# Four more pairs of tiles as seven products, parked attention outputs, and rooms of two lengths, in a one-layer decoder step

## The chip, the cores and the metric

The kernel runs on one core of a Trainium2 chip. The metric is the device time of one execution in microseconds: 1503.17 us, the median of 3 runs (1502.42 to 1503.85).

The engines are named as the profile names them: PE multiplies matrices into accumulators, PEld loads its weights, DVE is VectorE, ACT is ScalarE, POOL is GpSimd, and SP issues nearly all DMAs, in the order of the program.

## The reference

One layer for 528 prompt positions (16 meta tokens ahead of 512 tokens) and for 32 new tokens of eight running sequences: a half-step SwiGLU FFN, a mixer of gated linear attention and stick-breaking attention side by side, and a second half-step FFN, with RMS norms around each. Cut to what the change touches:

```python
h = x + 0.5 * rms_norm(swiglu(rms_norm(x, ffn1_pre_g), ffn1_w_gate, ffn1_w_up, ffn1_w_down), ffn1_post_g)
u = rms_norm(h, mix_pre_g)
q_a, k_a, v_a, gk_low, r_a, q_b, k_b, v_b, gate_a, gate_b = jnp.split(u @ w_in, offs, axis=-1)
o_a, s_new = gla_branch(q_a, k_a, v_a, g, s0, lead)
o_a = rms_norm(o_a, gla_norm_g).reshape(B, L, V_GLA) * jax.nn.silu(r_a)
o_b = sb_attend(q_b, keys, vals, sb_bias, q_off).reshape(B, L, SB_W)
m = jax.nn.sigmoid(gate_a) * (o_a @ w_o_gla) + jax.nn.sigmoid(gate_b) * (o_b @ w_o_sb)
h = h + rms_norm(m @ w_out, mix_post_g)
y = h + 0.5 * rms_norm(swiglu(rms_norm(h, ffn2_pre_g), ffn2_w_gate, ffn2_w_up, ffn2_w_down), ffn2_post_g)
```

The model width is 1024 and the FFN width 2816 (22 chunks of 128). Everything is float32.

## The kernel before

**Numbers.** Activations stand feature by token: tiles of 128 features by the tokens, in two halves of columns (280 + 280 in FFN1, 280 + 264 in the mixer as ordinary tiles, 272 + 272 in seven products). Each float32 operand is split into a high and a low part (`hi` on ACT, L661; `lo` = operand − `hi` on DVE, through the helper `tt` at L153), and each product is three matmuls: hi·hi, hi·lo, lo·hi.

**An ordinary tile** (`tile_steps`, L675 ff.) takes 128 output features of a weight matrix of 1024 rows: 8 steps, one for each chunk of 128 rows, of 6 matmuls (3 for each half of the columns). The FFN down tiles go by `k_steps` (L695 to L698) over 22 chunks in the three stretches `CUTS`, either with both halves of the columns or with one; a step of one half is 3 matmuls.

**Seven products** (`seven_steps`, L998; for the FFNs, L1188 and L1248) takes two tiles at once. The two tiles, the two halves of the 1024 rows and the two halves of the columns are a product of 2 by 2 blocks, done as seven block products and additions, with four accumulators: 14 steps of 6 matmuls. It needs sums of weight blocks (`weight_sums`, four sums of 512 columns on DVE), `hi` and `lo` of four quarter sets of weights (`parts_of`, `parted_lo`), sums of the activations (`usum`, in the mixer read back from `sums_dram` by `sums_back` and split by `sums_hi` and `sums_lo`), and additions that put the results together (`made`, `add`). `weights_at` puts the weight sums 10 to 8 steps ahead of a pair, and the quarters from 6 steps ahead to 6 steps into it. `gate_pair` does so for the gates `a` and `b`.

**The order is written by steps.** A matmul generator yields after each step, `step()` runs then, and whatever was put down by `later(d, f)` or `when(n, f)` for this step is issued behind it. So the lists of numbers (`F0`, `F1`, `SUMS_BACK`, `EARLY`, the pieces of `Weights`) set which instruction stands where on each engine.

**Weights** come by `st.fetch` (DMA on SP, L186; quarters for pairs, L621), asked up to `AHEAD` instructions before they are used, in the order of the list `st.todo`. `fetch_early` (L634) loads a piece of `w_in` ahead of the list, `h_again` (L1294) reads the residual back for the end of FFN1.

**The stages.** FFN1's gates and ups; FFN1 down by `order1`: tiles 0 and 1, the pair 2/3 ("S2"), then tiles 4 to 7 for the first half of the columns and 7 to 4 for the second; during the second the norms of the first half run (`g1.pieces`, delays `F0`), and after it those of the second half (`F1`). Their last part are the rank products `ranks` (L1667). Then nine stretches of 24 steps, in which attention pairs 0 to 7 and the four heads of the linear attention are worked off; in the ninth the gate tiles r0 to r2. The normed outputs of the linear attention (`oa`, eight tiles) stay in SBUF until the r tile with their number multiplies them by silu(r). Then the mixer by the list `MIXER`, whose steps are counted from its start: tiles r3 to r7, the products o0 to o7 (`out_a`, w_o_gla), gates a0 and a1 as ordinary tiles (`gate_a`), and the other a and b gates in pairs between the products p0 to p7. Between them stand the running sequences' attention over the cached pages: `Weights(0)` and `Weights(1)` make the attention weights of a half of the heads (a scan on DVE, L2174 ff., turned by PE, copied by DVE at L2199 and L2200), `sample_new` (L2229) uses them with the new values at step 9, and `sample_values` with the pages. Last come w_out and FFN2.

**Rooms.** `Arena` hands out stretches of SBUF. It has 25 chunks of 6 units of the same kind, and prefers the room that was given back longest ago by the count of gives. Pages of the cache come from a list of their own (`ring`).

## Time and profile before

| | |
|---|---|
| median of 3 runs | 1503.17 us |
| the profiled execution | 1503.28 us |
| its span | 1501.6 us, granted clock 0.999 |
| PE busy | 1492.8 us, 11941 instructions |
| DVE busy | 1090.2 us, 1940 instructions |
| ACT busy | 772.7 us, 1422 instructions |
| POOL busy | 73.4 us, 146 instructions |
| HBM read, written | 155.72 MB, 22.74 MB |

A time in a view is counted from the start of the span. A row of a timeline has start, length, engine, line, operation, output and input, and in brackets how long the engine stood idle before it and what ended that. A busy interval of PE covers the pipelined matmul (0.28 us and more), and neighbours overlap: the pitch from start to start is what one costs. A row of windows has for each engine busy time and the count of instructions, then the granted clock, the share of the DMA engines and GB/s.

### The profile page before, as it was taken

Reading aid. Unit: us, or ns where it says so; the run is one execution under the profiler, and the core shown is the slowest. Engines: PE = TensorE matmul, PEld = TensorE weight load, DVE = VectorE, ACT = ScalarE, POOL = GpSimd, SP = SyncE. Lnnn points to the kernel's source line nnn. Section 1 sums busy time; section 2 is a strip of 40 time slices with the busy share of each in tenths; the row PEclk is TensorE's granted clock in tenths of the full one; section 3 lists DMA queues with packets and bytes.
Section 4 is the critical chain, followed back from the end, with each engine's and each line's share of the span. In section 5 each row is a group of like instructions: output and inputs, shape, how many; then the busy total and the mean of one; then the engine's idle time right before and its main releaser. Section 6 shows DMA issues by size and latency. Waiting matters only on the chain.

```text
span 1501.6 us, 29825 instructions
## 1 busy us (share of the span) xinstructions
PE 1492.8 (99%) x11941; PEld 1442.1 (96%) x11941; DVE 1090.2 (73%) x1940; ACT 772.7 (51%) x1422; POOL 73.4 (5%) x146
## 2 busy tenths in 40 slices
PE   9999999999999999999999999999999999999998
PEld 8999999999999889999898999999999999999998
DVE  5888888853787866877776534977567898888544
ACT  6455454533655556556555443634564555455334
POOL 2000000000000011112111000000000000000000
PEclk9999999999999999999999999999999999999999
DMA  8133333337565474343555668335531333333253
GB/s 251 51 91 100 99 99 98 86 91 209 148 161 144 126 113 85 91 109 91 130 103 141 192 193 192 100 99 145 156 108 67 94 104 99 99 99 91 86 167 99
DMA packets 280525, 180.40 MB, mean 120 GB/s; under 512 B 10140, under 2 KB 260706, under 8 KB 280386
## 3 DMA queue, kind: packets, MB, share of 16 engines
q1 hardware_dynamic: 280082, 178.42, 44.0%
q8 instruction: 94, 1.54, 0.4%
q14 instruction: 45, 0.37, 0.1%
q0 software_dynamic: 288, 0.07, 0.0%
q10 hardware_dynamic: 16, 0.00, 0.0%
HBM read 155.72 MB, written 22.74 MB: 119 GB/s over the span
## 4 chain that ended last, share of the span: by engine, by line
PE 94%; DVE 3%; ACT 1%; DMA 1%; issue 0%; DVEq 0%; ACTq 0%; SPq 0%
PE acc L682 8%; PE acc L1248 8%; PE acc L1249 8%; PE acc L685 8%; PE acc L683 8%; PE acc L1250 8%; PE acc L695 7%; PE acc L698 7%; PE acc L696 7%; DVE room L153 2%; PE acc L1028 1%; PE acc L1029 1%; PE acc L1191 1%; PE acc L1030 1%; PE acc L1188 1%; PE acc L1189 1%
## 5 line engine op out<-in xcount | busy, mean ns | idle before, releaser
L153 DVE TENSOR_TENSOR lo<-raw,hi 128x1024 fp32r<-128x1024 f32 (+1 forms) x213 | 254.9, 1198 | 126.7 <-ACT hi L661 102.8
L153 DVE TENSOR_TENSOR room<-room,room 128x544 f32<-128x544 f32 (+17 forms) x413 | 259.1, 650 | 81.7 <-ACT room L761 14.0
L682 PE MATMUL acc<-room,hi 128*128 128x280 f32 (+1 forms) x928 | 271.7, 310 | 0.2 <-DVE room L156 0.2
L1248 PE MATMUL acc<-room,hi 128*128 128x280 f32 (+1 forms) x896 | 259.7, 290 | 0.0
L1249 PE MATMUL acc<-room,hi 128*128 128x280 f32 (+1 forms) x896 | 259.5, 290 | 0.0
L1250 PE MATMUL acc<-room,lo 128*128 128x280 f32 (+1 forms) x896 | 259.2, 289 | 0.0
L683 PE MATMUL acc<-room,hi 128*128 128x280 f32 (+1 forms) x928 | 250.8, 289 | 0.0
L685 PE MATMUL acc<-room,lo 128*128 128x280 f32 (+1 forms) x928 | 193.0, 289 | 0.0
L682 PEld LDWEIGHTS acc<-room,hi 128*128 128x128 f32 x928 | 174.7, 188 | 13.0 <-issue 11.0
L683 PEld LDWEIGHTS acc<-room,hi 128*128 128x128 f32 x928 | 175.2, 189 | 2.8 <-issue 1.9
L1250 PEld LDWEIGHTS acc<-room,lo 128*128 128x128 f32 x896 | 168.7, 188 | 0.0
L1249 PEld LDWEIGHTS acc<-room,hi 128*128 128x128 f32 x896 | 168.6, 188 | 0.0
L1248 PEld LDWEIGHTS acc<-room,hi 128*128 128x128 f32 x896 | 168.5, 188 | 0.0
L959 ACT CAST hi<-raw 128x1024 fp32r<-128x1024 f32 x92 | 96.4, 1052 | 133.6 <-PE acc L1249 49.2
L661 ACT CAST hi<-raw 128x1024 fp32r<-128x1024 f32 (+1 forms) x121 | 122.6, 1014 | 70.9 <-DMA raw<-in_ffn_w_down_dram 20.8
L685 PEld LDWEIGHTS acc<-room,lo 128*128 128x128 f32 x928 | 145.2, 189 | 0.0
L695 PE MATMUL acc<-room,hi 128*128 128x280 f32 (+2 forms) x498 | 142.9, 294 | 0.4 <-ACT hi L661 0.4
L696 PE MATMUL acc<-room,hi 128*128 128x280 f32 (+2 forms) x498 | 140.9, 290 | 0.0
L698 PE MATMUL acc<-room,lo 128*128 128x280 f32 (+2 forms) x498 | 127.8, 291 | 0.7 <-DVE lo L153 0.7
L959 ACT CAST hi<-room 128x1024 fp32r<-128x1024 f32 x84 | 70.2, 836 | 81.1 <-PE acc L1249 60.5
L695 PE MATMUL acc<-room,room 128*128 128x280 f32 (+3 forms) x366 | 107.8, 295 | 0.0
L153 DVE TENSOR_TENSOR lo<-room,hi 128x1024 fp32r<-128x1024 f32 x84 | 80.2, 955 | 36.8 <-ACT hi L959 36.6
(400 smaller groups left out, 3222.4 us busy)
## 6 DMA issues: line engine op xcount, KB each, us to landing
raw<-in_w_in_dram SPq DMA_DIRECT2D x49, 512.0 KB, 7.1
raw<-in_ffn_w_down_dram SPq DMA_DIRECT2D x40, 448.0 KB, 4.0
raw<-in_ffn_w_gate_dram SPq DMA_DIRECT2D x64, 256.0 KB, 3.2
raw<-in_ffn_w_up_dram SPq DMA_DIRECT2D x64, 256.0 KB, 3.2
out_dram<-room SPq DMA_DIRECT2D x36, 256.0 KB, 4.8
room<-in_cache_k_dram SPq DMA_DIRECT2D x32, 256.0 KB, 3.8
room<-in_cache_v_dram SPq DMA_DIRECT2D x32, 256.0 KB, 4.7
raw<-in_ffn_w_down_dram SPq DMA_DIRECT2D x14, 512.0 KB, 4.2
```

The lines of the kernel that those rows point to most:

```text
L153: (eng or V).tensor_tensor(out=out, in0=a, in1=b, op=op)
L661: S.copy(h_, src)
L682: T.matmul(acc[h][:, : wid[h]], hi[k], a[h][0], start=(k == 0), stop=False)
L683: T.matmul(acc[h][:, : wid[h]], hi[k], a[h][1], start=False, stop=False)
L685: T.matmul(acc[h][:, : wid[h]], lo[k], a[h][0], start=False, stop=(k == KD - 1))
L695: T.matmul(acc[h][:nw, : wid[h]], wh, a[h][0], start=(k == 0), stop=False)
L696: T.matmul(acc[h][:nw, : wid[h]], wh, a[h][1], start=False, stop=False)
L698: T.matmul(acc[h][:nw, : wid[h]], wl, a[h][0], start=False, stop=(k == kt - 1))
L959: S.copy(hi[:, :kt], src)
L1248: T.matmul(x[:, :QW], hi, act[k][0], start=(first and k == 0), stop=False, skip_group_check=True)
L1249: T.matmul(x[:, :QW], hi, act[k][1], start=False, stop=False, skip_group_check=True)
L1250: T.matmul(x[:, :QW], lo, act[k][0], start=False, stop=(k == 3), skip_group_check=True)
```

## The change

It does the following; how the order moves is shown at three places below.

- **Four more pairs as seven products.** In FFN1 down, tiles 4 and 5 ("S4" in `order1`), right behind the pair 2/3; of its 22 chunks, eight go as seven products, the others as before. In the mixer, r3/4 and r5/6 (the new `r_pair`) and the gates a0/1 (`gate_pair`; `gate_a` is gone).
- **The mixer's order.** `MIXER` now begins 24 steps earlier in its own count, with r0, r1, r2 in the last of the nine stretches; then r7, the two r pairs, o0 to o3, a0/1, o4, o5, a2/3, o6, o7, and the rest. The first product o0 reads its eight inputs in the order 0, 1, 2, 7, 3, 4, 6, 5.
- **The sums of the activations** (`sums_back`) are read back and split during attention pairs 5 to 8 instead of at steps 80 to 104 of the mixer. The first half of the full tiles of u is given back in parts when r3/4 begins.
- **Parking.** Each head of the linear attention stores its two outputs in `oa_dram` and gives their rooms back; r0, r1, r2 and r7 load theirs when they begin, an r pair 6 steps after it begins (`oa_back`).
- **FFN1 down's end.** Only tiles 6 and 7 are left as single ones. `F0` and `LATE` have other delays, the early piece of `w_in` goes from tile 4 to tile 7, and `h_again` starts 14 steps after pair 4/5 (pieces of another size) instead of 2 steps after pair 2/3.
- **Weights(0)** has its scans two steps and its turning and copies three steps later. The 16 small copies of `sample_out` go from DVE to ACT. The loads of `ob` and of pages have fixed steps.
- **Rooms.** 20 chunks of 6 units and the rest of 2; a room freed 14 steps ago or more is preferred; pages use the same rooms.

In the programs, PE has 48 matmuls less (11398 to 11350). DVE has 37 two-operand instructions more and the 16 copies less, SP 18 DMAs more (575).

PE, at step 8 of the mixer. In both programs the rows of `ps` are `sample_new(0)`, ahead of it are the last of the tile before and one step of the next. Before:

```order
L685 MATMUL acc_9609<-room_20_279,lo_9400 128x280
L685 MATMUL acc_9610<-room_20_279,lo_9400 128x264
L682 MATMUL acc_9716<-room_15_160,hi_9533 128x280
L683 MATMUL acc_9716<-room_15_160,hi_9533 128x280
L682 MATMUL acc_9717<-room_15_160,hi_9533 128x264
L683 MATMUL acc_9717<-room_15_160,hi_9533 128x264
L685 MATMUL acc_9716<-room_15_160,lo_9534 128x280
L685 MATMUL acc_9717<-room_15_160,lo_9534 128x264
L2229 MATMUL ps_9726<-room_7_72,room_52_5498 32x128 x4
L2229 MATMUL ps_9726<-room_7_72,room_50_5418 32x128 x4
```

Now:

```order
L689 MATMUL acc_9659<-room_24_154,lo_9586 128x280
L689 MATMUL acc_9660<-room_24_154,lo_9586 128x264
L1033 MATMUL acc_9789<-room_43_3190,hi_9689 128x272
L1034 MATMUL acc_9789<-room_32_329,hi_9689 128x272
L1035 MATMUL acc_9789<-room_43_3190,lo_9690 128x272
L1033 MATMUL acc_9789<-room_32_329,hi_9689 128x272
L1034 MATMUL acc_9789<-room_32_329,hi_9689 128x272
L1035 MATMUL acc_9789<-room_32_329,lo_9690 128x272
L2233 MATMUL ps_9804<-room_78_5427,room_6_71 32x128 x4
L2233 MATMUL ps_9804<-room_78_5427,room_75_5331 32x128 x4
```

Tile r4 began here, with two accumulators; now the pair r3/4 begins, with the first of four, after r7.

DVE, ahead of the same place: from the low part of the tile before to the second copy of turned attention weights (L2200, now L2203), which `sample_new(0)` reads. Before, without the four small ones of the second scan:

```order
L153 TENSOR_TENSOR lo_9534<-raw_9134,hi_9533 128x1024
L156 SCALAR_TENSOR_TENSOR room_45_5239<-room_45_5239,newm 128x32
L2174 TENSOR_SCALAR room_45_5239<-room_45_5239 128x32
L2175 SCALAR_TENSOR_TENSOR room_45_5239<-room_45_5239 128x288
L153 TENSOR_TENSOR room_51_5461<-room_51_5461,newm 128x32
L153 TENSOR_TENSOR room_51_5461<-room_51_5461,room_45_5239 128x287
L153 TENSOR_TENSOR room_66_9545<-room_6_71,room_20_279 128x544
...
L2200 COPY room_52_5498<-ps_9601 32x128
...
L2200 COPY room_50_5418<-ps_9640 32x128
```

Now:

```order
L153 TENSOR_TENSOR lo_9586<-raw_9070,hi_9585 128x1024
L153 TENSOR_TENSOR room_61_4651<-raw_9467,raw_9177 128x512
L153 TENSOR_TENSOR raw_9177<-raw_9177 128x512
L156 SCALAR_TENSOR_TENSOR room_55_4248<-room_55_4248,newm 128x32
...
L153 TENSOR_TENSOR room_61_4651<-raw_9467,raw_9177 128x512
L153 TENSOR_TENSOR room_54_4247<-raw_9467,room_61_4651 128x512
...
L153 TENSOR_TENSOR lo_9690<-raw_9177,hi_9689 128x1024
...
L2203 COPY room_6_71<-ps_9704 32x128
...
L2203 COPY room_75_5331<-ps_9734 32x128
```

Between the low part of the tile and the copies now stand the four weight sums of r3/4 (512 columns) and the low part of its first quarters (`lo_9690`).

SP, behind FFN1 down's last pair, from its last quarters on. The rows of `h_dram` are `h_again`, the row of `in_w_in` is the early piece. Before, behind pair 2/3:

```order
L621 DMA raw_3512<-in_ffn_w_down_dram 128x4x128 x2
L186 DMA raw_3568<-in_ffn_w_down_dram 128x8x128
L186 DMA raw_3675<-in_ffn_w_down_dram 128x7x128
L186 DMA raw_3725<-in_ffn_w_down_dram 128x7x128
L1294 DMA room_39_3857<-h_dram 128x560
L634 DMA room_38_3839<-in_w_in_dram 128x4x256
L1294 DMA room_39_3857<-h_dram 128x560
L186 DMA raw_3795<-in_ffn_w_down_dram 128x8x128
L1294 DMA room_39_3857<-h_dram 128x560
L186 DMA raw_3833<-in_ffn_w_down_dram 128x7x128
```

Now, behind pair 4/5:

```order
L625 DMA raw_3863<-in_ffn_w_down_dram 128x4x128 x2
L186 DMA raw_3917<-in_ffn_w_down_dram 128x8x128
L186 DMA raw_4024<-in_ffn_w_down_dram 128x7x128
L186 DMA raw_4074<-in_ffn_w_down_dram 128x7x128
L1299 DMA room_55_4248<-h_dram 128x560
L1299 DMA room_54_4247<-h_dram 128x560 x2
L186 DMA raw_4144<-in_ffn_w_down_dram 128x8x128
L638 DMA room_57_4283<-in_w_in_dram 128x4x256
L186 DMA raw_4182<-in_ffn_w_down_dram 128x7x128
L186 DMA raw_4191<-in_ffn_w_down_dram 128x7x128
```

Before, two loads of the residual and the early piece stand ahead of tile 5's first chunk (`raw_3795`); now three loads of the residual stand ahead of tile 7's (`raw_4144`), and the early piece behind it.

The diff, cut to its core:

```diff
 RE_FFN = 3
 U_SUMS = (5, 6, 9)
-KEEP = 5
-SUMS_BACK = (80, 88, 96, 104)
-MIXER = [("R", "r", n) for n in range(3, 8)]
-MIXER += [("R", "o", n) for n in range(8)] + [("R", "a", 0), ("R", "a", 1), ("S", "b", 0), ("S", "a", 2), ("S", "b", 2), ("R", "p", 0), ("R", "p", 1)]
-MIXER += [("S", "a", 4), ("R", "p", 2), ("R", "p", 3), ("S", "b", 4), ("S", "a", 6), ("R", "p", 4), ("R", "p", 5), ("S", "b", 6)]
-MIXER += [("R", "p", 6), ("R", "p", 7)]
+SUMS_BACK = (-85, -61, -37, -20)
+MIXER = [("R", "r", 0), ("R", "r", 1), ("R", "r", 2), ("R", "r", 7), ("S", "r", 3), ("S", "r", 5)]
+MIXER += [("R", "o", n) for n in range(4)] + [("S", "a", 0), ("R", "o", 4), ("R", "o", 5), ("S", "a", 2), ("R", "o", 6), ("R", "o", 7)]
+MIXER += [("S", "b", 0), ("S", "a", 4), ("R", "p", 0), ("R", "p", 1), ("S", "b", 2), ("R", "p", 2), ("R", "p", 3), ("S", "a", 6), ("S", "b", 4)]
+MIXER += [("R", "p", 4), ("R", "p", 5), ("S", "b", 6), ("R", "p", 6), ("R", "p", 7)]
 AHEAD = 150
 LEAVE = 12
-SPREAD = 15
-UNITS = 150
+UNITS, LONGS = 150, 20
...
-                since = max(f) if not empty else max(free) + SPREAD
+                other = empty and self.tile[c] is not None and self.tile[c].dtype != dt
+                since = max(free) if other else max(f)
                 waste = k % 2 == 0 and s % 2
                 alone = k == 1 and free[s ^ 1] is not None
-                key = (empty and empties <= self.keep, waste, tight and sum(x is not None for x in free), alone, since)
+                opens = empty and long and k <= self.SHORT
+                key = (opens and spare <= self.RESERVE, waste, self.now - since < self.RECENT, opens, alone, since)
                 if best is None or key < best[0]:
                     best = (key, c, s)
         assert best is not None, f"no room for {width}: {[sum(x is not None for x in f) for f in self.freed]}"
...
+    oa_dram = dp.tile([8, P, NP + NS], F32, name="oa_dram")
...
+                for e in range(2):
+                    later(1, lambda e=e: nc.sync.dma_start(oa_dram[2 * hd + e], oa[hd, e]))
+                    later(6, lambda e=e: give(oa.pop((hd, e))))
...
-    def tile_steps(act, w1):
+    def tile_steps(act, w1, order=range(KD)):
-        for k in range(KD):
+        for k in order:
...
-    GATES, ROWS, EARLY = 6, 1, {4: 2}
-
-    F0, F1 = (5, 13, 20), (5, 11, 14)
+    GATES, ROWS, EARLY = 6, 1, {7: 2}
+
+    F0, F1 = (4, 10, 14), (5, 11, 14)
-    LATE, MIX = (12, 22), (2, 4)
+    LATE, MIX = (18, 22), (2, 4)
...
-    order1 = [(0, (0, 1)), (1, (0, 1)), "S2"] + [(n, (0,)) for n in range(4, 8)] + [(n, (1,)) for n in range(7, 3, -1)]
+    order1 = [(0, (0, 1)), (1, (0, 1)), "S2", "S4"] + [(n, (0,)) for n in range(6, 8)] + [(n, (1,)) for n in range(7, 5, -1)]
...
-                down1.pair(n, ("ps", "acc"), True)
-                later(2, lambda: h_again(8))
+                down1.pair(n, ("ps", "acc") if n == 2 else ("acc", "ps"), n == 4)
+                if n == 4:
+                    later(14, lambda: h_again(6))
                 continue
...
-                accs[n, hs] = {h: ps("acc") for h in hs}
+                accs[n, hs] = {h: ps("ps" if (n, hs) == (6, (0,)) else "acc") for h in hs}
...
-                if (n, hs) == ((7, (0,)), (4, (1,)))[h]:
+                if (n, hs) == ((7, (0,)), (6, (1,)))[h]:
...
-        t = ring.pop(0)
+        t = take(512)
...
-        def pieces(self, n):
+        def pieces(self, n, d=0):
+            e = d and d - 1
             return ((n + 4, self.rooms), (n + 1, self.new), (n + 2, lambda: self.sigmoids(0)), (n + 3, lambda: self.sigmoids(1)),
-                    (n + 3, lambda: self.scan(0)), (n + 5, lambda: self.scan(1)), (n + 6, lambda: self.turn(0)),
-                    (n + 7, lambda: self.out(0)), (n + 8, lambda: self.turn(1)), (n + 9, lambda: self.out(1)))
+                    (n + 3 + e, lambda: self.scan(0)), (n + 5 + e, lambda: self.scan(1)), (n + 6 + d, lambda: self.turn(0)),
+                    (n + 7 + d, lambda: self.out(0)), (n + 8 + d, lambda: self.turn(1)), (n + 9 + d, lambda: self.out(1)))
 
...
-                V.tensor_copy(ob[pr][r_, NP : NP + NS].rearrange("p (b t) -> p b t", t=4),
+                S.copy(ob[pr][r_, NP : NP + NS].rearrange("p (b t) -> p b t", t=4),
                               p[r_, 64 * pr : 64 * pr + 64].rearrange("p (b e t) -> p b e t", e=2, t=4)[:, :, e])
...
+    def oa_back(n):
+        o = take(NW)
+        nc.sync.dma_start(o, oa_dram[n])
+        return o
...
 
+        o = oa_back(n)
         acc = yield from tile_steps(um, W1)
-        sg, o = take(NW), oa[n // 2, n % 2]
+        sg = take(NW)
...
+    def r_pair(n):
+
+        o, t, sg, outs = {}, {}, {}, {}
+        q0, q1 = slice(0, QW), slice(QW, NW)
+
+        def load():
+            for i in range(2):
+                o[i] = oa_back(n + i)
+
+        def second():
+            t[1] = take(NW)
+            outs.update(c12=t[1][:, q0], c22=t[1][:, q1])
+
+        def first():
+            t[0] = take(NW)
+            outs.update(c11=lambda a: S.copy(t[0][:, q0], a), c21=t[0][:, q1])
+
+        def by_t(i):
+            sg[i] = take(NW)
+            S.activation(sg[i], t[i], AF.Sigmoid)
+            tt(o[i], o[i], t[i], ALU.mult)
+
+        def by_sg(i):
+            tt(o[i], o[i], sg[i], ALU.mult)
+            give(t[i], sg[i])
+            split(oas, n + i, o[i], oap)
+
+        for d, f in ((6, load), (10, second), (11, first), (14, lambda: by_t(1)), (15, lambda: by_sg(1)), (16, lambda: by_t(0)),
+                     (17, lambda: by_sg(0))):
+            later(d, f)
+        yield from seven_steps(("r", n), usum, QW, outs)
...
-        acc = yield from tile_steps(oas, W1)
+        acc = yield from tile_steps(oas, W1, (0, 1, 2, 7, 3, 4, 6, 5) if n == 0 else range(KD))
...
-            for h in range(2):
+            for h in range(1 if k < 4 else 2):
...
+        starts, n = {}, -24
+        for i, (kind, what, t) in enumerate(MIXER):
+            starts[what, t] = n
+            if kind == "S":
+                weights_at(when, n, (what, t))
+            elif i > 1:
+                when(n - 5, st.split)
+                when(n - 4, st.fetch)
+            n += 14 if kind == "S" else 8
+        for d in (-5, -1):
+            when(n + d, st.split)
+            when(n + d + 1, st.fetch)
+        for i in range(4):
+            when(SUMS_BACK[i], sums_back, i)
+            for m in range(2):
+                when(SUMS_BACK[i] + 6 + 4 * m, sums_hi, i, m)
+                when(SUMS_BACK[i] + 8 + 4 * m, sums_lo, i, m)
+
+        def halved():
+            for k in range(4):
+                parts_ = [arena.halves(t) for t in um.full[k]]
+                give(*(t[1] for t in parts_))
+                um.full[k] = [t[0] for t in parts_]
+
+        when(starts["r", 3], halved)
+
+        def product_b(n):
+            acc = yield from tile_steps(obs, W1)
...
-                then(17, lambda: todo.extend([n, f] for n, f in w0.pieces(1)))
+                then(17, lambda: todo.extend([n, f] for n, f in w0.pieces(1, 3)))
...
+            if pr > 4:
+                for n in range(24 * pr - 216 + 1, 24 * pr - 192 + 1):
+                    for f, args in mixer_at.pop(n, ()):
+                        then(n + 216 - 24 * pr, f, *args)
...
-            for main in (now.queries, now.keys, now.values) if now else (lambda i=i: gate_r(i) for i in range(3)):
+            for main in (now.queries, now.keys, now.values) if now else (lambda: islice(mixer, 24),):
...
-            when(starts["b", 0] + 2 + 4 * i, lambda i=i: split(obs, i, ob[i], obp))
+            when(118 + 4 * i, lambda i=i: split(obs, i, ob[i], obp))
...
-            when(starts["a", 0] + 2 + i, ob_back, i)
+            when(102 + i, ob_back, i)
```

121 lines of the change are left out of this document (45 added, 76 removed).

## The prediction, made before the change was run

> **What bounds the kernel now.** I read the head of the page and the chain that ended last, then the waits of TensorE, then windows where TensorE runs plain, and last the timeline at every place where it does not.
>
> ```profile
> span 1501.6 us, 29825 instructions
> PE 1492.8 (99%) x11941; PEld 1442.1 (96%) x11941; DVE 1090.2 (73%) x1940; ACT 772.7 (51%) x1422; POOL 73.4 (5%) x146
> ...
> PE 94%; DVE 3%; ACT 1%; DMA 1%; issue 0%; DVEq 0%; ACTq 0%; SPq 0%
> ```
>
> PE is busy for 99% of the span and makes 94% of the chain. The waits show how little is left beside its own work (microseconds in total, times, longest):
>
> ```profile
> PE acc L1476 <- DVE own L256: 1.1, 1, 1.1
> PE acc L698 <- DVE lo L153: 0.7, 1, 0.7
> ...
> PE acc L695 <- ACT hi L661: 0.4, 1, 0.4
> ...
> PE acc L1028 <- DVE room L153: 0.4, 1, 0.4
> ```
>
> Each happens once. So the kernel is a stream of matmuls at a fixed pitch, with a few holes under 2 us. A change pays by matmuls taken out and by holes closed; everything else it does is free only while it opens no hole. The pitch comes from windows that are full of matmuls of one width (busy and count of PE first):
>
> ```profile
> 150.00:200.00 50.00, 50.00 (x390) 50.00 (x389) 43.94 (x66) 23.92 (x37) 0.00 (x0) 1.00 0.33 96
> 1200.00:1250.00 50.00, 50.00 (x402) 50.00 (x401) 45.37 (x69) 26.45 (x41) 0.00 (x0) 1.00 0.36 106
> ```
>
> The first is FFN1, whose matmuls have 280 columns: 50/389 = 128.5 ns each, start to start. The second is FFN2 with 272: 50/402 = 124.4 ns. The granted clock is 1.00 in both. A mean of 290 ns in a group of the page would count the overlap of neighbours, so I don't use it.
>
> **The matmuls that go.** An ordinary tile takes 8 steps of 6, a pair 96. As seven products a pair takes 14 steps of 6, 84. FFN1 down's pair 4/5 has 22 chunks in three stretches, and the instruction counts of the two programs give 12 fewer there as well, so four pairs make 48 fewer (11398 to 11350). The 12 of FFN1 down are 12 × 128.5 ns = 1.54 us, the 36 of r3/4, r5/6 and a0/1 are 36 × 124.4 ns = 4.48 us. Together **−6.02 us**. Since PE is never idle for long, all of it shows if the products' additions keep up.
>
> The page "TensorE: Matmul & The Clock Gate" of the Trainium skill, section "Back-to-back issue gap", holds that weight load and matmul together set the sustained spacing, about 81 ns at 128 columns and 131 ns at 512. Drawn straight between these (an estimate), 272 to 280 columns would cost about 100 ns and the 48 matmuls 4.8 us. The rows above show 124 to 128 ns, and by them the term stays as it is.
>
> **The hole in FFN1 down** lies where tile 5 begins, one half tile behind pair 2/3.
>
> ```profile
> 342.50 0.29 PE L698 MATMUL acc<-room,lo 128*128 128x280 f32 x1
> 343.18 0.41 PE L695 MATMUL acc<-room,hi 128*128 128x280 f32 x1 [0.39 <-ACT hi L661]
> 343.43 0.29 PE L696 MATMUL acc<-room,hi 128*128 128x280 f32 x1
> 344.44 0.40 PE L698 MATMUL acc<-room,lo 128*128 128x280 f32 x1 [0.73 <-DVE lo L153]
> ...
> 334.14 7.87 DMA raw<-in_ffn_w_down_dram
> ...
> 342.08 1.05 ACT L661 CAST hi<-raw 128x1024 fp32r<-128x1024 f32 x1 [4.80 <-DMA raw<-in_ffn_w_down_dram]
> ...
> raw<-in_ffn_w_down_dram SPq DMA_DIRECT2D x40, 448.0 KB, 4.0
> ...
> 331.48 0.34 SPq L1294 DMA_DIRECT2D room<-h_dram  x1
> 331.87 0.43 SPq L634 DMA_DIRECT2D room<-in_w_in_dram  x1
> ...
> 350.00:355.00 5.00, 5.00 (x41) 5.00 (x41) 2.05 (x2) 1.14 (x2) 0.00 (x0) 1.00 1.07 331
> ```
>
> Start to start, 342.50 to 343.18 is 0.55 us over the pitch and 343.43 to 344.44 is 0.88 us over it: 1.43 us. The first weights of tile 5 were issued at 334.14 and landed 7.87 us later, where this group's median is 4.0: two loads of the residual (L1294) and the early piece of `w_in` (L634) went out just ahead of them, from 331.48 on, and a little later the DMA engines move 331 GB/s. After the change the same place is where tile 7 begins, behind pair 4/5. SP's order there has three loads of the residual ahead of the first weights, and the early piece behind them. A load waits on SP for its room alone. The residual's rooms are taken 14 steps behind the pair, and by the new rule they are ones freed 14 steps before that, about at the pair's end or sooner, so these loads can be on their way before the weights. With 4.0 instead of 7.87 us the weights land 3.9 us sooner, against a hole of 1.43. I take the hole as gone: **−1.43 us** (to 0, if the three loads go out just ahead as well). The reader that comes next is tile 7, beside the residual.
>
> **The hole in the mixer** lies between three pairs in a row.
>
> ```profile
> 963.92 0.28 PE L1030 MATMUL acc<-room,lo 128*128 128x272 f32 x1
> 964.56 0.39 PE L1028 MATMUL acc<-room,hi 128*128 128x272 f32 x1 [0.36 <-DVE room L153]
> ...
> 954.93 8.10 DMA raw<-in_w_in_dram
> ...
> 965.00:970.00 5.00, 5.00 (x42) 5.00 (x41) 5.00 (x8) 3.23 (x6) 0.00 (x0) 1.00 0.36 106
> ...
> 941.73 3.25 DVE L2250 COPY room<-ps 64x32 f32<-64x32 f32 x16
> ```
>
> It costs 964.56 − 963.92 − 0.124 = 0.52 us; VectorE is busy 5.00 of 5.00 us there, and has just spent 3.25 us on small copies. After the change the copies are ScalarE's (busy 3.23 of 5), the eight low parts of the sums are made during the attention, and at most two pairs stand together. I take **−0.52 us** (0 to −0.52). The additions that VectorE gains (37 instructions in the whole program) come with the new pairs and are weighed next.
>
> **A new hole at the start of the mixer.** Here VectorE gets the weight sums of r3/4 ahead of the turned attention weights that `sample_new(0)` on PE reads at step 9, in both programs.
>
> ```profile
> 834.85 0.27 DVE L2200 COPY room<-ps 32x128 f32<-32x128 f32 x1
> ...
> 838.99 0.57 PE ps L2229 x16
> ...
> 951.21 0.69 DVE L153 TENSOR_TENSOR room<-raw,room 128x512 f32<-128x512 f32 x1
> 951.93 0.44 DVE L153 TENSOR_TENSOR room<-room,acc 128x272 f32<-128x272 f32 x1
> 952.29 0.72 DVE L153 TENSOR_TENSOR room<-room,room 128x544 fp32r<-128x544 f32 x1
> 952.92 0.43 DVE L153 TENSOR_TENSOR room<-room,acc 128x272 f32<-128x272 f32 x1
> 953.27 1.22 DVE L153 TENSOR_TENSOR lo<-raw,hi 128x1024 fp32r<-128x1024 f32 x1
> 954.40 0.44 DVE L153 TENSOR_TENSOR room<-room 128x272 f32<-128x272 f32 x1
> ```
>
> Before, the copy ends at 835.12, 3.9 us ahead of its reader. The starts of the block below it give the price of one instruction when VectorE runs full: a sum of 512 columns 0.72 us, an addition from an accumulator 0.36, one of 544 columns 0.63, a low part of 1024 columns 1.13. Ahead of the copy now stand four weight sums (2.9 us) and one more low part (1.13): 835.12 + 4.0 = 839.1, and with 0.4 us for the ScalarE results between them 839.5. That is 0.5 us behind 838.99. The turning itself moves two to three steps later, so PE may also wait for the scans in a step of 0.75 us, twice. I take **+0.6 us** (0 to +1.6). Behind this wait on PE stand the sample products and the rest of r3/4, nothing on another engine.
>
> Behind it VectorE stays full through both r pairs. From step 9 to the split of r5/6's outputs (step 42) the order gives it 8 low parts, 10 operations of 512, 14 of 544 and 12 of 272 columns: 9.0 + 7.2 + 8.8 + 4.3 = 29.3 us.
>
> ```profile
> 873.73 0.41 PE L685 MATMUL acc<-room,lo 128*128 128x280 f32 x2
> ```
>
> PE reaches step 42 at 873.7, 34.7 us after step 9. So 84% of the time is spoken for; I add nothing, and come back to it among the rivals. The same holds for attention pairs 5 to 8, which get the sums back (two low parts of 544 columns for each, 1.3 us of VectorE in a stretch of some 31):
>
> ```profile
> 620.00:650.00 30.00, 30.00 (x228) 27.65 (x227) 23.70 (x60) 17.22 (x35) 5.49 (x15) 1.00 0.31 83
> ```
>
> 23.7 + 1.3 of 30 leaves 5 us. The 16 loads and stores of parked outputs (280 KB or so each) land in stretches with a DMA share of a third to two thirds, asked six steps ahead or more: nothing. Rooms of two lengths and the spread of the page loads change who waits for whose room, and by their rule a room is taken 14 steps after it was freed where there is one: nothing.
>
> **A new hole at the end of FFN1 down.** With two halves of tiles left over instead of four, the norm of the first half of the columns has 44 steps of 3 matmuls to run in, 17.0 us, where it had 34. How long such a norm takes is seen in the second half, which had no more room before:
>
> ```profile
> 408.40 0.63 PE L757 MATMUL ps<-room,ones 128*128 128x280 f32 x2
> ...
> 410.53 2.11 DVE L153 TENSOR_TENSOR room<-room,room 128x840 f32<-128x840 f32 x2 [4.46 <-ACT room L761]
> ...
> 425.53 1.51 DVE L153 TENSOR_TENSOR room<-room,room 128x560 f32<-128x560 f32 x2
> ...
> 426.94 1.08 PE ps L1667 x16
> ```
>
> From 408.40 to the last addition (427.04) it takes 18.6 us, and the rank product at 426.94 is just met. By its steps (4, 10, 14) the first half's rank product now comes at about 17.9 us after the end of its accumulation: 0.7 us short, of which the order of the additions gives some back and ScalarE's two late results take some. I take **+0.6 us** (0 to +1.6).
>
> **The sum** goes against the profiled execution, 1503.28 us with a span of 1501.6; it stands 0.1 us above the median of 1503.17. 1503.28 − 6.02 − 1.43 − 0.52 + 0.6 + 0.6 = 1496.5, so **1496.4 us** by the median: 0.45% faster. A measurement of this kernel can tell about 0.2% (3.0 us) from no change.
>
> **The rivals.**
>
> *The old holes stay* and only move: the DMA burst meets tile 7, VectorE is as full in two pairs as in three. For it: the same bytes and nearly the same additions are in the same microseconds. Against it: FFN2 down has the two pairs in this order already, and its window shows no hole (401 matmuls in 50 us are 124.7 ns each):
>
> ```profile
> 1400.00:1450.00 50.00, 50.00 (x401) 50.00 (x400) 22.51 (x32) 15.68 (x24) 0.00 (x0) 1.00 0.35 100
> ```
>
> The time would be 1496.4 + 1.43 + 0.52 = 1498.3.
>
> *VectorE becomes the bound around the r pairs.* If its 29.3 us came with waits on ScalarE and PE of a fifth (5.9 us) they would fill the 34.7, and each further microsecond would be PE's, in r7's accumulators and in the first product that reads the outputs 5 and 6. With both new holes at 1.6 and 2 us more: 1496.4 + 2.0 + 2.0 = 1500.4, on the edge of what can be told. For it: DVE 5.00 of 5.00 in the pairs of before. Against it: three such pairs together cost only 0.52.
>
> *Transfers collide in the mixer.* Pages, parked outputs, `ob` back and quarters all go through SP in order. One late load like that of 343 in front of a reader costs 1.4 us, two 2.9: 1499.3.
>
> The page "DMA: Bandwidth & Descriptors" of the Trainium skill, section "Specifications", gives about 358 GB/s for the memory of one core. By it the 331 GB/s of the row above has little left, and parking adds traffic; the sums here don't need it.
>
> *Slower: SP stands still for a room.* A load into a room waits on SP for the room's last reader, and every weight load behind it waits too; parking puts such loads ahead of the quarters of both r pairs. The chunk issued at 954.93 took 8.10 us and landed 1.5 us before it was wanted (964.56). An SP wait that costs a whole such load is 8.1 − 1.5 = 6.6 us of PE, twice 13.2: 1509.6. It makes the kernel slower once both waits together pass 1506.2 − 1496.4 = 9.8 us of PE, 6.4 us each on SP. Against it: the rooms are picked 14 steps (10 us) after they were freed.
>
> *The change doesn't do what it says* would mean matmuls that stay; the counts exclude it, and no chance goes to it.
>
> **How the numbers follow.** Forecast 0.62, old holes stay 0.15, VectorE 0.11, transfers 0.07, SP 0.05. Best case of the forecast: no new hole, 1495.2, and 0.7 us of other small waits gone, 1494.5. The range is 1494.3 to 1500.3. Faster by over 0.2% (below 1500.2) are the first two whole, 0.06 of VectorE and 0.05 of the transfers: 0.88. Within it are 0.05 of VectorE, 0.02 of the transfers and 0.01 of SP: 0.08. Slower is the rest of SP: 0.04.
>
> **What would show it.** Right: 48 fewer matmuls at the same pitch; no wait of FFN1 down's half tiles for `lo` or `hi` behind pair 4/5; no wait of the gate pairs `a` and `b` for VectorE; a wait of `sample_new`'s first matmul for VectorE of about half a microsecond, and one at the rank product of the first half. Wrong: PE waits for VectorE in o0 or in r7's evacuation, for `hi` behind a DMA in the r pairs, or a DMA issue on SP with long idle time ahead of it.

## The result, and the profile after

The changed kernel takes **1494.84 us** (median of 6 runs, 1493.88 to 1496.08) where the kernel before takes 1503.32 (6 runs): a ratio of 0.9944, with a 95% interval of 0.9932 to 0.9957. The forecast was 1496.4, its range 1494.3 to 1500.3. So the sign and the range held, and 1.6 us more went than the sum had. The profiled execution took 1495.05 us.

The head and the chain of the page, after:

```profile
span 1493.4 us, 29839 instructions
...
PE 1484.9 (99%) x11893; PEld 1434.2 (96%) x11893; DVE 1105.0 (74%) x1961; ACT 778.9 (52%) x1445; POOL 68.3 (5%) x146
...
PE 95%; DVE 3%; ACT 1%; issue 1%; DVEq 0%; ACTq 0%
```

PE has 48 instructions less and stays at 99%. The transfers have left the chain. The four longest waits of PE after (us in total, times, longest):

```profile
PE acc L1480 <- DVE own L257: 1.1, 1, 1.1
PE acc L830 <- DVE room L153: 0.4, 1, 0.4
PE ps L2233 <- DVE room L2203: 0.4, 1, 0.4
PE ps L1561 <- DVE room L1560: 0.4, 1, 0.4
```

The waits for `lo` and `hi` in FFN1 down and the one of the gate pairs are gone. L2233, `sample_new`, is new, where the prediction had put it.

Where the time went is read from one instruction in both profiles, at the end of each stage:

| up to | before | after | difference | of this stage | forecast for it |
|---|---|---|---|---|---|
| end of FFN1's gates and ups | 278.27 | 277.71 | −0.56 | −0.56 | 0 |
| end of FFN1 down and its norms (L912, now L917) | 433.49 | 430.90 | −2.59 | −2.03 | −2.37 |
| attention, late in the ninth stretch (L682, now L686) | 823.59 | 820.75 | −2.84 | −0.25 | 0 |
| mixer, w_out and into FFN2 (L698, now L702) | 1094.84 | 1086.75 | −8.09 | −5.25 | −4.40 |
| last matmuls (L825, now L830) | 1496.26 | 1487.36 | −8.90 | −0.81 | 0 |

The two stages that the change rewrites gave 7.28 us, where 6.77 were forecast. Another 1.62 came from stages in which no matmul was changed. The span shrinks by less than the last row, 8.2 us: the profiled execution has 5.7 us behind its last matmul, where every other profile of this case has 4.9 to 5.4. So the span of another run understates what it loses on PE against this profile, by 0.3 to 0.8 us.

### The profile page after: what moved, and what is told of

Its sections match the earlier page's. It is cut to its first block, busy times and chain, and to the rows that moved or that the text cites. A ratio compares the mean times of both kernels' runs of the same rounds, so it can differ in the third digit from the quotient of the medians.

```text
span 1493.4 us, 29839 instructions
## 1 busy us (share of the span) xinstructions
PE 1484.9 (99%) x11893; PEld 1434.2 (96%) x11893; DVE 1105.0 (74%) x1961; ACT 778.9 (52%) x1445; POOL 68.3 (5%) x146
## 4 chain that ended last, share of the span: by engine, by line
PE 95%; DVE 3%; ACT 1%; issue 1%; DVEq 0%; ACTq 0%
PE acc L1253 8%; PE acc L1254 8%; PE acc L1255 8%; PE acc L686 7%; PE acc L687 7%; PE acc L689 7%; PE acc L699 6%; PE acc L702 6%; PE acc L700 6%; PE acc L1033 2%; PE acc L1034 2%; PE acc L1035 2%; PE acc L1196 1%; PE acc L1193 1%; DVE room L153 1%; PE acc L1194 1%
## 5 line engine op out<-in xcount | busy, mean ns | idle before, releaser
L153 DVE TENSOR_TENSOR room<-room,room 128x544 fp32r<-128x544 f32 (+16 forms) x424 | 263.3, 643 | 71.3 <-ACT room L766 16.6
L1253 PE MATMUL acc<-room,hi 128*128 128x280 f32 (+1 forms) x896 | 259.5, 290 | 0.0
L1254 PE MATMUL acc<-room,hi 128*128 128x280 f32 (+1 forms) x896 | 259.1, 289 | 0.0
L1255 PE MATMUL acc<-room,lo 128*128 128x280 f32 (+1 forms) x896 | 258.9, 289 | 0.0
L686 PE MATMUL acc<-room,hi 128*128 128x280 f32 x832 | 244.4, 310 | 0.2 <-DVE room L156 0.2
L687 PE MATMUL acc<-room,hi 128*128 128x280 f32 x832 | 225.2, 289 | 0.0
L689 PE MATMUL acc<-room,lo 128*128 128x280 f32 x832 | 172.9, 289 | 0.0
L1254 PEld LDWEIGHTS acc<-room,hi 128*128 128x128 f32 x896 | 168.6, 188 | 0.0
L1255 PEld LDWEIGHTS acc<-room,lo 128*128 128x128 f32 x896 | 168.6, 188 | 0.0
L1253 PEld LDWEIGHTS acc<-room,hi 128*128 128x128 f32 x896 | 168.6, 188 | 0.0
L686 PEld LDWEIGHTS acc<-room,hi 128*128 128x128 f32 x832 | 156.7, 188 | 12.0 <-issue 10.0
L687 PEld LDWEIGHTS acc<-room,hi 128*128 128x128 f32 x832 | 157.1, 189 | 2.8 <-issue 1.9
L665 ACT CAST hi<-raw 128x1024 fp32r<-128x1024 f32 (+1 forms) x107 | 108.2, 1012 | 73.8 <-issue 23.9
L689 PEld LDWEIGHTS acc<-room,lo 128*128 128x128 f32 x832 | 130.2, 188 | 0.0
L699 PE MATMUL acc<-room,hi 128*128 128x280 f32 (+2 forms) x388 | 110.8, 295 | 0.0
L153 DVE TENSOR_TENSOR room<-room,acc 128x272 f32<-128x272 f32 (+1 forms) x180 | 76.3, 436 | 45.6 <-PE acc L1035 22.8
L700 PE MATMUL acc<-room,hi 128*128 128x280 f32 (+2 forms) x388 | 108.8, 290 | 0.0
```

The costliest lines, as they stand in the source:

```text
L153: (eng or V).tensor_tensor(out=out, in0=a, in1=b, op=op)
L665: S.copy(h_, src)
L686: T.matmul(acc[h][:, : wid[h]], hi[k], a[h][0], start=(k == order[0]), stop=False)
L687: T.matmul(acc[h][:, : wid[h]], hi[k], a[h][1], start=False, stop=False)
L689: T.matmul(acc[h][:, : wid[h]], lo[k], a[h][0], start=False, stop=(k == order[-1]))
L699: T.matmul(acc[h][:nw, : wid[h]], wh, a[h][0], start=(k == 0), stop=False)
```

## The experiments

Each kernel is one of the two with one edit. Its gain or loss is read at the place of the edit, by the start of the same instruction in two profiles, since small differences elsewhere (below) reach a microsecond.

### Does the pitch belong to the execution or to the program?

FFN1's gates and FFN2 run the same instructions before and after, and became shorter. Both kernels were profiled a second time, and the kernel before got another constant in the choice of rooms:

```diff
-SPREAD = 15
+SPREAD = 20
```

> The kernel before once more, for the pitch of the stages that the change leaves alone (FFN1's gates and ups, 45 to 270 us: 0.6 us longer before than after; FFN2, 1130 to 1480 us: 0.8 us longer before than after). Theory A (the pitch drifts from execution to execution): FFN1's stretch differs from the first profile of this kernel by 0.2 to 0.8 us. Theory B (the pitch belongs to the program, by where its rooms lie): the two profiles agree within 0.1 us over each stretch, and the 1.4 us belong to the change.

> The changed kernel once more, for the same question. Theory A: FFN2's stretch differs from its first profile by 0.2 to 0.8 us. Theory B: within 0.1 us. By the executions timed so far its span should be 1491.9 to 1493.9.

> The kernel before with another constant in the choice of rooms (SPREAD 20 for 15): the same instructions on each engine but for merged waits, other rooms from FFN1 on. Theory B (the pitch of the matmuls belongs to the placement of the rooms): the stretch from 100 to 260 us or that of FFN2 (1180 to 1340 us) changes its mean pitch by 0.2 ns or more against 129.04 and 125.18 ns, without waits. Rival (it belongs to something else in the program): both stay within 0.05 ns, as in two runs of the same kernel.

Windows over the middle of FFN1 and of FFN2 (busy and count of PE first). The kernel before, and its second profile:

```profile
100.00:260.00 160.00, 160.00 (x1242) 160.00 (x1242) 139.43 (x208) 79.96 (x121) 0.00 (x0) 1.00 0.33 96
1180.00:1340.00 160.00, 160.00 (x1281) 160.00 (x1280) 142.65 (x216) 81.77 (x125) 0.00 (x0) 1.00 0.34 100
```

```profile
100.00:260.00 160.00, 160.00 (x1242) 160.00 (x1241) 139.41 (x208) 80.02 (x121) 0.00 (x0) 1.00 0.33 96
1180.00:1340.00 160.00, 160.00 (x1281) 160.00 (x1280) 142.67 (x216) 81.79 (x125) 0.00 (x0) 1.00 0.34 100
```

With the other rooms, and then the changed kernel:

```profile
100.00:260.00 160.00, 160.00 (x1248) 160.00 (x1247) 139.42 (x208) 80.65 (x122) 0.00 (x0) 1.00 0.34 97
1180.00:1340.00 160.00, 160.00 (x1279) 160.00 (x1278) 142.39 (x216) 81.74 (x127) 0.00 (x0) 1.00 0.34 100
```

```profile
100.00:260.00 160.00, 160.00 (x1246) 160.00 (x1246) 138.63 (x209) 80.53 (x122) 0.31 (x1) 1.00 0.34 97
1180.00:1340.00 160.00, 160.00 (x1284) 160.00 (x1283) 141.62 (x215) 80.17 (x123) 0.00 (x0) 1.00 0.35 102
```

In 160 us PE is never idle in any of them, and the clock is 1.00. Yet 1242, 1242, 1248 and 1246 matmuls fall into the window of FFN1, and 1281, 1281, 1279 and 1284 into that of FFN2. These counts include the two or three that reach over its edges. From start to start a matmul took 129.04 ns in FFN1 in both profiles of the kernel before, 128.49 with the other rooms and 128.56 in the changed kernel; in FFN2 125.18, 125.32 and 124.85. (The 128.5 and 124.4 ns of the prediction were counted with those at the edges, and so are 0.4 to 0.6% low; over 48 matmuls that is 0.04 us.) The two profiles of one kernel agree to the matmul; from start to start, theirs stay within 0.2 us of each other over the whole span behind the first 10 us, in both pairs. The kernel before with other rooms gains 0.7 us in FFN1 and loses 0.55 in FFN2. So theory B holds: the pitch belongs to the program, and **the choice of rooms alone** moves it by up to half a nanosecond on average, 0.5 to 1 us over FFN1's 2100 or FFN2's 3200 matmuls. In the runs below, FFN2 alone takes up to 1.0 us longer than in the changed kernel, as a drift and not as a jump, and in three of them its length is the same to 0.01 us. Whether it is the addresses of the operands that cost time, or something that other rooms bring along, was not looked into.

### The hole in FFN1 down

```diff
-                if n == 4:
-                    later(14, lambda: h_again(6))
+                if n == 4:
+                    later(2, lambda: h_again(8))
...
-    GATES, ROWS, EARLY = 6, 1, {7: 2}
+    GATES, ROWS, EARLY = 6, 1, {6: 2}
```

> The changed kernel with the residual read back from two steps behind pair 4/5 in pieces of the old size and the early piece of w_in at tile 6: two loads of the residual and the early piece stand right ahead of tile 7's first weights, as they stood ahead of tile 5's in the kernel before. Theory (that burst made the hole of 1.43 us): the weights land 6 to 8 us after their issue, PE waits for them where tile 7 begins for 0.8 to 1.7 us in all, span 1494.2 to 1495.1. Rival (the hole went with the place, not with the order of the loads): no wait there, span 1493.4 within 0.3.

The timeline of this kernel where tile 7 begins, PE, then SP, then ACT:

```profile
375.00 0.40 PE L699 MATMUL acc<-room,hi 128*128 128x280 f32 x1 [0.49 <-ACT hi L665]
376.26 0.40 PE L702 MATMUL acc<-room,lo 128*128 128x280 f32 x1 [0.74 <-DVE lo L153]
...
363.56 0.43 SPq L638 DMA_DIRECT2D room<-in_w_in_dram  x1
...
365.84 0.37 SPq L186 DMA_DIRECT2D raw<-in_ffn_w_down_dram  x1
...
373.90 1.05 ACT L665 CAST hi<-raw 128x1024 fp32r<-128x1024 f32 x1 [4.92 <-DMA raw<-in_ffn_w_down_dram]
```

The hole is back, with the same two waits. From start to start PE falls 1.77 us back between 374.22 and 376.49; the kernel before lost 1.67 there, counted in the same way, with the slow restarts behind both waits. The weights issued at 365.84 are ready for ACT at 373.90, 8.1 us later. The changed kernel, SP and ACT at the same place:

```profile
363.26 1.29 SPq L1299 DMA_DIRECT2D room<-h_dram  x3
365.91 0.38 SPq L186 DMA_DIRECT2D raw<-in_ffn_w_down_dram  x1
366.34 0.58 SPq L638 DMA_DIRECT2D room<-in_w_in_dram  x1
...
370.27 1.05 ACT L665 CAST hi<-raw 128x1024 fp32r<-128x1024 f32 x1 [1.22 <-DMA raw<-in_ffn_w_down_dram]
```

Three loads of the residual go out from 2.65 us ahead of the weights on, and the weights still take 4.4 us. In the kernel before and in this run the first load of the residual has the same lead, 2.66 us, so the lead is not what changed.

The edit moves the residual and the early piece together, but the trace of this run tells them apart. The load of the residual that went out ahead of the early piece (363.18) landed after 2.7 us; the one right behind it (364.04) took 8.0, as the weights did. The packets of the three kinds have different sizes: 2240 bytes for the residual, 1024 for the early piece, 512 for the weights. The first packet of the weights starts at 369.60, when most of the early piece's 512 packets (from 364.93 to 370.90) have started, and just before that the DMA engines are far from full (the last two numbers are their share and GB/s):

```profile
366.00:369.00 3.00, 3.00 (x25) 3.00 (x25) 2.50 (x6) 2.88 (x6) 0.00 (x0) 1.00 0.26 94
```

In the changed kernel the first packet of the weights starts at 366.98, 1.1 us after the issue, and the early piece's at 368.96; the weight chunks behind the early piece take 6.3 to 6.9 us there, too. So 2.7 of the 3.7 us by which the weights land later pass before their first packet, behind the early piece and with the DMA engines a quarter busy. A burst that fills them, as the 331 GB/s of the prediction suggest, comes after that and can make up the rest at most. No run moves the early piece alone.

The place has little slack: at the next chunk, at 377.8, the changed kernel itself loses 0.16 us, and the runs below that have the same order of SP lose up to 0.66 us more there.

### The hole in the mixer

```diff
-                V.tensor_copy(ob[pr][r_, NP : NP + NS].rearrange("p (b t) -> p b t", t=4),
+                S.copy(ob[pr][r_, NP : NP + NS].rearrange("p (b t) -> p b t", t=4),
```

> The kernel before with the 16 small copies of the running sequences' outputs on ScalarE instead of VectorE (3.25 us at 941.73). Theory (VectorE carries these copies into three pairs in a row): the hole of 0.52 us at 964 is gone, nothing else changes but pitch; span 1501.6 - 0.5 = 1501.1, give or take 0.1. Rival (three pairs in a row fill VectorE by themselves): a hole of 0.3 to 0.5 us is left there.

The kernel before with this edit alone, at the hole:

```profile
964.16 0.40 PE L1028 MATMUL acc<-room,hi 128*128 128x272 f32 x1 [0.20 <-DVE room L153]
```

PE gains 0.42 us in all, but only 0.16 of it here: from start to start 0.36 us of the hole of 0.52 are left, which is the rival's number. The other 0.26 us are gained at 953.41, where the kernel before loses as much in two starts, without a wait long enough for a row. And VectorE isn't full right ahead of 964; it stands idle for weights that have not landed. First the kernel before, then this one:

```profile
959.39 0.69 DVE L153 TENSOR_TENSOR room<-raw,raw 128x512 f32<-128x512 f32 x1 [0.31 <-DMA raw<-in_w_in_dram]
...
963.12 0.69 DVE L153 TENSOR_TENSOR room<-raw,room 128x512 f32<-128x512 f32 x1 [0.35 <-DMA raw<-in_w_in_dram]
```

```profile
959.06 0.69 DVE L153 TENSOR_TENSOR room<-raw,raw 128x512 f32<-128x512 f32 x1 [0.34 <-DMA raw<-in_w_in_dram]
...
962.72 0.69 DVE L153 TENSOR_TENSOR room<-raw,room 128x512 f32<-128x512 f32 x1 [0.27 <-DMA raw<-in_w_in_dram]
```

The addition that PE waits for follows without a gap behind the last of these rows. Without the 0.35 and 0.27 us of idle time it would have ended that much sooner, and PE's waits were 0.36 and 0.20. So by the trace what is left of this hole hangs on late weights at the third pair. (The window of the prediction in which VectorE is busy 5.00 of 5.00 us lies behind the hole, from 965 on; from 959 to 964 it is busy 4.27.) In the changed kernel, with two pairs in a row, both holes are gone, although VectorE stands idle for such a load there, too (1.99 us until 940.49). So late weights cost PE nothing there; whether earlier weights alone would close the hole of the kernel before was not tested.

### What a pair is worth

```diff
-("S", "a", 0), ("R", "o", 4)
+("R", "a", 0), ("R", "a", 1), ("R", "o", 4)
...
-        when(starts["r", 3], halved)
+        when(starts["a", 2], halved)
```

(with `gate_a` of the kernel before), and for r5 and r6:

```diff
-("S", "r", 3), ("S", "r", 5)]
+("S", "r", 3), ("R", "r", 5), ("R", "r", 6)]
...
-        when(starts["r", 3], halved)
+        when(starts["a", 0], halved)
```

> The changed kernel with the gates a0 and a1 as two ordinary tiles, as before the change (96 matmuls for 84). Theory (a pair is worth its matmuls): from the end of o3 to the end of FFN2 12 matmuls more, 96 x 125.8 ns - 84 x 124.4 ns = 1.6 us longer, span 1494.6 to 1495.4. Rival (the pair's additions cost PE part of it): 0.5 to 1.1 us longer.

> The changed kernel with r5 and r6 as two ordinary tiles. Theory (a pair is worth its matmuls, and VectorE keeps up with two r pairs in a row): 1.6 us longer between the start of r5 and o7, no wait of PE goes; span 1494.6 to 1495.4. Rival (two r pairs in a row fill VectorE and cost PE part of it): less than 1.1 us longer.

Two ordinary tiles in place of a0/1 make the stretch around them 1.42 us longer (0.58 us late at 909.5, 2.00 at 1038.2), in place of r5/6 1.55 us (0.08 to 1.63). That is the price of 12 matmuls, and no wait of PE comes or goes at the place with either: the additions of the pairs cost PE nothing, and VectorE keeps up with two r pairs in a row. By the last matmul the two kernels are 2.95 and 2.34 us behind the changed one (spans 1495.6, over the range expected, and 1495.0); the rest is FFN2's pitch (1.0 and 0.8) and, in the first, 0.65 us at the chunk of 377.8.

### The wait of `sample_new`

Four kernels went at it. The weight sums one step earlier:

```diff
-        for i, d in enumerate((-10, -10, -9, -8)):
+        for i, d in enumerate((-11, -11, -10, -9) if f == ("r", 3) else (-10, -10, -9, -8)):
```

> The changed kernel with the four weight sums of the pair r3/4 one step earlier, so that two of them stand ahead of the low part of r7, where VectorE was idle for 3.35 us. Theory (VectorE's order makes the wait of 0.41 us at the first new-value product): the wait is gone, the second eight of its matmuls start 0.3 us behind the first, and PE gains 0.6 us there. Rival (the turned weights themselves come late from PE or ScalarE): wait of 0.3 to 0.6 us as before, no gain.

The wait stayed at 0.4 us. Two sums did move ahead of r7's low part, but VectorE's idle 3.35 us is spent at the instruction ahead of both, which waits for ScalarE, so nothing moved into it. This run doesn't tell the two apart.

```diff
-                then(17, lambda: todo.extend([n, f] for n, f in w0.pieces(1, 3)))
+                then(17, lambda: todo.extend([n, f] for n, f in w0.pieces(1, 0)))
```

> The changed kernel with the scans, turnings and copies of Weights(0) at the steps they had before the change. Theory (VectorE is full from the low part of r7 on): the copies end over 1 us before the first new-value product, but the low part of r3/4's first quarters now stands behind them and PE waits for it 0 to 0.6 us at the pair's start; gain 0 to 0.6 us. Rival (the later steps were needed for nothing else, and VectorE is not full): no wait of PE at either place, gain 0.6 us.

Here both were wrong: the wait at L2233 is gone, but PE loses 1.7 us between 826 and 840. PE and VectorE in this kernel:

```profile
828.03 0.52 PE L689 MATMUL acc<-room,lo 128*128 128x280 f32 x2 [0.55 <-DVE lo L153]
831.14 0.41 PE L2188 MATMUL ps<-ident,room 128*128 128x128 f32 x2 [1.40 <-DVE room L153]
...
824.43 0.19 DVE L156 SCALAR_TENSOR_TENSOR room<-room,newm 128x32 f32<-128x32 f32 x1 [4.33 <-ACT room L2171]
```

The first scan now stands on VectorE ahead of its ScalarE input, and everything behind it, r7's low part too, waits with it. The later steps of the change are needed.

```diff
+        if f == ("r", 3) and n < 2:
+            if n == 0:
+                S.copy(t3, b22)
+            return
         tt(*((t3, b22, t1), (t1, t1, b11), (t2, b22, t1), (t4, b21, t2))[n], ALU.subtract)
```

> The changed kernel without two of the four weight sums of r3/4 on VectorE: one is replaced by a plain copy on ScalarE, one is left out, so r3 and r4 and what follows from them hold other values. VectorE has 1.33 us less ahead of the copies of the turned weights, and nothing else waits in their place. Theory (VectorE's queue alone makes the wait at the first new-value product): the second copy ends 1.0 to 1.4 us earlier (836.59 in the changed kernel), the wait of 0.41 us is gone and PE gains 0.5 to 0.6 us from there to the end of o0; span 1492.8, give or take 0.5 for the start. Rival (the turning on PE or ScalarE's part comes late, too): the wait stays at 0.2 us or more.

The copies and their reader, in the changed kernel:

```profile
836.32 0.27 DVE L2203 COPY room<-ps 32x128 f32<-32x128 f32 x1
...
835.90 0.42 PE L2233 MATMUL ps<-room,room 64*32 64x128 f32 x8
836.74 0.42 PE L2233 MATMUL ps<-room,room 64*32 64x128 f32 x8 [0.41 <-DVE room L2203]
```

and with two sums less:

```profile
835.62 0.27 DVE L2207 COPY room<-ps 32x128 f32<-32x128 f32 x1
...
836.49 0.64 PE L2237 MATMUL ps<-room,room 64*32 64x128 f32 x16
```

Against PE the copy ends 1.3 us earlier (0.69 us behind the first product's start before, 0.60 ahead of it now), the 16 products run as one group, and PE is 0.6 us further. VectorE's queue alone made this wait.

### The rank products

At the end of FFN1 down the waits show nothing, and yet 1.1 us was lost there. The rank products on PE before, and then after with the VectorE addition that they read:

```profile
405.28 1.15 PE L1667 MATMUL ps<-room,room 128*32 128x280 f32 x16
...
426.87 1.15 PE L1667 MATMUL ps<-room,room 128*32 128x280 f32 x16
```

```profile
401.17 1.75 PE L1672 MATMUL ps<-room,room 128*32 128x280 f32 x16
...
423.80 1.63 PE L1672 MATMUL ps<-room,room 128*32 128x280 f32 x16
...
400.68 1.51 DVE L153 TENSOR_TENSOR room<-room,room 128x560 f32<-128x560 f32 x2
...
423.19 1.51 DVE L153 TENSOR_TENSOR room<-room,room 128x560 f32<-128x560 f32 x2
```

The last addition ends at 402.19, and by the trace's single records the last two of the eight products start at 402.25; in the second half at 424.70 and 424.76. So PE waits for VectorE, but between the passes of a group of small matmuls, whose earlier ones still run: no idle time, and no row among the waits. The test moves the products back:

```diff
-            ranks(h)
+            later(2, lambda h=h: ranks(h))
...
-    LATE, MIX = (18, 22), (2, 4)
+    LATE, MIX = (20, 24), (2, 4)
```

> The changed kernel with both rank products two half steps later on PE (and what follows them two steps later). Theory (VectorE's last addition of the norm is late, so the rank product stands still between its passes): each of the two rank groups takes 1.03 to 1.15 us again instead of 1.75 and 1.6, and the span falls by about 1.0 us, 1493.4 to 1492.4. Rival (the groups are long because of where their operands lie in SBUF, or their shape): they stay at 1.6 to 1.75 us and the span stays at 1493.4 within 0.3.

Both groups take 1.15 us again, so the theory holds for the groups. The span doesn't follow: 1495.2. What is behind the second group in this kernel, PE and then ACT:

```profile
429.92 0.66 PE L1680 MATMUL ps<-room,sel 128*32 128x280 f32 x2 [1.60 <-ACT room L1676]
...
429.15 0.42 ACT L1616 CAST room<-room 128x280 fp32r<-128x280 f32 x1 [1.63 <-DVE room L156]
429.48 0.38 ACT L1676 COPY room<-ps 128x280 f32<-128x280 f32 x1
```

The copy of the ranks (L1676) now stands on ScalarE behind a cast that waits for VectorE, and the sum on PE waits 1.6 us for it. From start to start PE gains 0.6 and 0.7 us at the two groups, and loses 0.5 behind the first, 1.8 with this wait, and 0.65 at 439.9, where a product waits 0.40 us for VectorE (L222): 1.7 us lost in all. The chunk at 377.8 took another 0.66 us here, the start of the kernel 0.9 (a wait for VectorE until 19.03).

The last try put both cures together, the ranks moved less and two sums of r3/4 on GpSimd:

```diff
-            ranks(h)
+            later(1 + h, lambda h=h: ranks(h))
...
-            later(2, copied)
+            later(2 - h, copied)
...
-        tt(*((t3, b22, t1), (t1, t1, b11), (t2, b22, t1), (t4, b21, t2))[n], ALU.subtract)
+        tt(*((t3, b22, t1), (t1, t1, b11), (t2, b22, t1), (t4, b21, t2))[n], ALU.subtract, G if f == ("r", 3) and n < 2 else None)
```

(`LATE` is (19, 24) here.)

> The changed kernel with two edits at places far apart. (1) The rank products one and two half steps later, the copy of the second one a step sooner behind it than in late_rank. Theory: both groups take 1.15 us, 1.0 us less in sum, and PE waits less than 0.3 us for the copy (1.6 us in late_rank, where ScalarE stood at another instruction ahead of it). Rival: the wait for the copy comes back at 0.5 us or more. (2) Two of the four weight sums of r3/4 on GpSimd. Theory (VectorE's queue makes the wait at the first new-value product): VectorE's copies end 1.0 to 1.4 us earlier against PE, the wait is gone, PE gains 0.6 us there. Rival (the turned weights come late from elsewhere, or the third sum waits for GpSimd): 0.3 us or less gained. Together a span of 1491.4, give or take 0.8 for what the placement of the rooms does to FFN2's pitch; time 1493.3.

Its time is 1497.44 us (median of 5, 1496.33 to 1500.79), 0.9966 of the kernel before (0.9952 to 0.9979). The two intervals overlap a little, but each of its five runs is longer than all six of the change (at most 1496.08). Its first rank group takes 1.37 us, its second 1.15. Of its waits of PE:

```profile
PE ps L1680 <- ACT room L1676: 1.8, 1, 1.8
...
PE ps L2188 <- DVE room L153: 0.7, 1, 0.7
PE ps L2233 <- DVE room L2203: 0.4, 1, 0.4
```

The copy of the ranks comes too late again, and the loss at 439 is there as well; PE is 2.0 us behind from then on. And the sums on GpSimd cost more than they freed: PE waits 0.7 us for the scan ahead of the turning and falls 0.9 us back, and the wait at L2233 stays. The timeline of GpSimd and VectorE there:

```profile
826.01 1.37 POOL L153 TENSOR_TENSOR room<-raw,raw 128x512 f32<-128x512 f32 x1
827.46 2.15 POOL L153 TENSOR_TENSOR raw<-raw 128x512 f32<-128x512 f32 x1
...
826.14 2.32 DVE L153 TENSOR_TENSOR lo<-raw,hi 128x1024 fp32r<-128x1024 f32 x1
828.39 1.27 DVE L156 SCALAR_TENSOR_TENSOR room<-room,newm 128x32 f32<-128x32 f32 x1
```

Apart from the kernel that leaves two sums out, nothing tried here beats the changed kernel. Of four runs that went for 0.6 to 1.6 us at these two places, one gained nothing and three lost 1.7, 1.7 and 2.9 us there.

## Why the prediction was right, point by point

- **The matmuls, −6.02 us: right.** An ordinary pair of tiles in place of seven products costs 1.42 and 1.55 us, against 1.49 forecast for 12 matmuls; FFN1 down's own pair was not undone.
- **The hole in FFN1 down, −1.43: right**, and the order of the loads is its cause (residual_early brings it back). With the restarts 1.67 us went, and 0.16 at 377.8 is left of it. The reason given was not the one: the prediction set its hope on the residual's loads being on their way before the weights, and was ready for 0 if they go out just ahead. They had the same lead of 2.7 us before and after; what the weights no longer stand behind is the early piece.
- **The hole in the mixer, −0.52: right that it goes, the cause only in part.** The copies were 0.16 of it, and 0.26 of another hole at 953.41 that was not in the sum. The rest, by the trace, hung on VectorE's idle time for late weights, which the prediction did not have. It has "at most two pairs stand together" as well, and that may be what closes the rest, since the weights come late after the change, too; no run tells the two apart.
- **The new hole at `sample_new`, +0.6: right** in place, cause and size: the copy was forecast 0.5 us behind its reader, and ended 0.69 us behind the first product; PE lost 0.6.
- **The new hole at the end of FFN1 down, +0.6: right in place and cause, too small.** The first half lost 0.6 us as forecast (1.75 for 1.15). The second half, for which nothing was added because its delays stayed, lost 0.5 us: VectorE came into it with the rest of the first half's norm, and its last addition ended 0.7 us later against PE than before (0.90 us behind the start of the group, 0.17 before). That VectorE was late is shown by late_rank, the reason for it is read from the timeline alone.
- **The step that was mis-sized** is the one that put the rooms at nothing. They were weighed as waits only, and as waits they did cost nothing. But the pitch went with them: −0.56 us in FFN1, −0.81 in FFN2, and in the mixer ordinary tiles went from 125.6 to 125.2 ns a matmul (mean from start to start in both profiles), about 0.4 us over the 850 of the changed kernel. That rooms alone do this is shown in the kernel before (SPREAD); for these three places it is argued from that. With these 1.7 us, 0.4 more from the holes of the mixer, 0.1 more from that of FFN1 down, and 0.5 back for the second rank group, the 6.77 us of the sum come to 8.5; the two profiles differ by 8.9 at the last matmul. Of the 0.4 that remain, 0.25 lie in the attention, and are not explained. Both new holes came, and yet the measured 1494.84 lies below the 1495.2 that the forecast had for no new hole; that it is still inside the range was luck, owed to 0.7 us set aside for other small waits.
- **The rivals.** Old holes that stay: no, but for the 0.16 us at 377.8. VectorE as the bound around the r pairs: no, no PE wait from r7 to o0 beside `sample_new`. Transfers, and SP at a stand: no wait of PE for one after the change, beside that chunk. By the spacing of about 100 ns that was drawn from the page "TensorE: Matmul & The Clock Gate" of the Trainium skill, section "Back-to-back issue gap", a pair would be worth 1.2 us; 1.42 and 1.55 were measured.

## What to carry to other kernels

When PE is busy for 99% of the time, count matmuls and holes, and look for each hole at the order of the engine that ends it: an instruction that waits there takes all that stands behind it along. A full engine can be late for other reasons than its own work, so look at what it stood idle for just ahead of the hole, and not only at how busy it is around it. When a load is late, look at which transfer stands ahead of it in its queue, and whether the DMA engines were full meanwhile. Groups of small matmuls hide a wait, since they count as busy; compare their length with the same group in another profile. And before a difference of a microsecond in a stage that wasn't touched is explained, profile both kernels twice and move the buffers once.
